# The head rows of batch 0 through two hardware DMA queues in a rotary-embedding kernel

## The chip, the cores and the metric

The kernel runs on one core of a Trainium2 chip. A core has compute engines that run their own instruction streams (VectorE, ScalarE, GpSimd, also called POOL, and SyncE, also called SP, which only issues transfers and waits; TensorE isn't used here) and 16 DMA engines that move data between the device memory (DRAM) and the on-chip memory (SBUF, 128 partitions). An engine's instruction stream issues a transfer into its queue and goes on; the DMA engines do the moving. The metric is the device time of one launch in microseconds (us), the median of several runs.

## The reference

The kernel applies a rotary position embedding. `x` is 8 x 2048 x 16 x 64 (batch, sequence, heads, head size), float32, 67.1 MB; `cos` and `sin` are 2048 x 32, 0.26 MB each. The output has the shape and type of `x`.

```python
x1 = x[..., :head_dim // 2]
x2 = x[..., head_dim // 2:]
cos = cos[None, :, None, :]
sin = sin[None, :, None, :]
out1 = x1 * cos - x2 * sin
out2 = x1 * sin + x2 * cos
return np.concatenate([out1, out2], axis=-1)
```

## The kernel before

One batch is one tile. The 2048 positions lie on 128 partitions, `J` = 16 consecutive positions ("rows" of 16 x 64 values) on each, so a partition's share of a batch is one contiguous piece of 64 KB in DRAM. Tiles are float16: a load through POOL's queue (line 52) casts float32 to float16 on the way, and a store (lines 60, 100, 130, 132) casts back. [...] There are five tile buffers for eight batches.

The first two rows of batch 0 (`JA` = 2) take another way. They come in as float32 through SP's queue into the tile `head`, 128 partitions x 8 KB (line 36), and ScalarE copies them, cast, into the first tile (line 84). The load of batch 0 on POOL's queue brings rows 2 to 15 alone. Behind the head, SP's queue carries `sin` and `cos` (lines 44 and 45), 2 KB per partition each. ScalarE turns sin into float16 with both signs (lines 88 and 89) and cos into float16 (line 90).

`rotate` is three VectorE instructions on a stretch of rows: the products of the swapped halves with sin into `v` (line 73), the products with cos in place (line 79), and their sum (line 81). It runs for rows 0 and 1 of batch 0 first, then rows 2 to 15, then for the seven other batches.

The order in POOL's queue is partly written out with dependencies between instructions: the loads of batches 0 to 3, then the store of row 0 of batch 0 (line 100), then the load of batch 4, the store of the rest of batch 0 (line 60), and from there stores and the loads of batches 5 to 7. A load into a used buffer waits for the store of what lay in it. Transfers of one queue take their turn in the order of issue on each DMA engine.

The last batch leaves in three parts: rows 0 to 8 (line 130) and 9 to 13 (line 132) through POOL's queue, and the last two rows through SP's: ScalarE copies them to float32 in `head`, used a second time (line 140), and SP stores them (line 141) once the part of line 130 has landed.

The change touches lines 36 to 39 of the kernel before. ScalarE's instruction stream there has six instructions that count as work and issues no transfer.

Of the kernel before, what the change touches and what calls it, by code (L numbers as in the profile page):

```python
# [1 line left out]

# [4 lines left out]


@with_exitstack  # L10
def kernel(
    ctx: ExitStack,
    tc: tile.TileContext,
    x: bass.AP,
    cos: bass.AP,
    sin: bass.AP,
    out: bass.AP,
):
    nc = tc.nc
    f16 = mybir.dt.float16  # L20
    f32 = mybir.dt.float32

    B, S, H, D = x.shape
    Dh = D // 2
    P = nc.NUM_PARTITIONS
    J = S // P
    NBUF = 5

    const_pool = ctx.enter_context(tc.tile_pool(name="rope_const", bufs=1))
    io_pool = ctx.enter_context(tc.tile_pool(name="rope_io", bufs=NBUF))  # L30
    tmp_pool = ctx.enter_context(tc.tile_pool(name="rope_tmp", bufs=1))

    JA = 2
    head = const_pool.tile([P, JA, H, D], f32)
    x0 = x[0].rearrange("(p j) h d -> p j (h d)", j=J)
    nc.sync.dma_start(  # L36
        out=head.rearrange("p j h d -> p (j h d)"),
        in_=x0[:, 0:JA, :].rearrange("p j f -> p (j f)"),
    )
    sin_f = const_pool.tile([P, J, Dh], f32)  # L40
    cos_f = const_pool.tile([P, J, Dh], f32)
    cos_h = const_pool.tile([P, J, Dh], f16)
    sin_h = const_pool.tile([P, J, D], f16)
    nc.sync.dma_start(out=sin_f, in_=sin.rearrange("(p j) d -> p j d", j=J))  # L44
    nc.sync.dma_start(out=cos_f, in_=cos.rearrange("(p j) d -> p j d", j=J))

    loads = []

    def load(b):
        xt = io_pool.tile([P, J, H, D], f16)  # L50
        j0 = JA if b == 0 else 0
        dma = nc.gpsimd.dma_start(  # L52
            out=xt[:, j0:J, :, :].rearrange("p j h d -> p (j h d)"),
            in_=x[b].rearrange("(p j) h d -> p j (h d)", j=J)[:, j0:J, :].rearrange("p j f -> p (j f)"),
        )
        loads.append(dma)
        return xt

    def store(b, xt, j0=0):
        return nc.gpsimd.dma_start(  # L60
            out=out[b].rearrange("(p j) h d -> p j (h d)", j=J)[:, j0:J, :].rearrange("p j f -> p (j f)"),
            in_=xt[:, j0:J, :, :].rearrange("p j h d -> p (j h d)"),
        )

    def rotate(xt, j0, j1):
        v = tmp_pool.tile([P, J, H, D], f16)
        n = j1 - j0
        js = slice(j0, j1)
        shape = [P, n, H, 2, Dh]
        sin_b = sin_h[:, js, :].rearrange("p j (e d) -> p j e d", e=2).unsqueeze(2).to_broadcast(shape)  # L70
        cos_b = cos_h[:, js, :].unsqueeze(2).to_broadcast([P, n, 2 * H, Dh])
        xe = xt[:, js, :, :].rearrange("p j h (e d) -> p j h e d", e=2)
        nc.vector.tensor_mul(  # L73
            out=v[:, js, :, :].rearrange("p j h (e d) -> p j h e d", e=2),
            in0=xe[:, :, :, ::-1, :],
            in1=sin_b,
        )
        xw = xt[:, js, :, :].rearrange("p j h (e d) -> p j (h e) d", d=Dh)
        nc.vector.tensor_mul(out=xw, in0=xw, in1=cos_b)  # L79
        xa = xt[:, js, :, :].rearrange("p j h d -> p (j h d)")  # L80
        nc.vector.tensor_add(out=xa, in0=xa, in1=v[:, js, :, :].rearrange("p j h d -> p (j h d)"))  # L81

    tiles = [load(b) for b in range(NBUF - 1)]
    nc.scalar.copy(  # L84
        out=tiles[0][:, 0:JA, :, :].rearrange("p j h d -> p (j h d)"),
        in_=head.rearrange("p j h d -> p (j h d)"),
    )
    nc.scalar.copy(out=sin_h[:, :, Dh:D], in_=sin_f)  # L88
    nc.scalar.mul(out=sin_h[:, :, 0:Dh], in_=sin_f, mul=-1.0)  # L89
    nc.scalar.copy(out=cos_h, in_=cos_f)  # L90
    rotate(tiles[0], 0, JA)
    def part(b, j0, j1):
        return (
            out[b].rearrange("(p j) h d -> p j (h d)", j=J)[:, j0:j1, :].rearrange("p j f -> p (j f)"),
            tiles[b][:, j0:j1, :, :].rearrange("p j h d -> p (j h d)"),
        )

    def store_rows(b, j0, j1):
        dst, src = part(b, j0, j1)
        return nc.gpsimd.dma_start(out=dst, in_=src)  # L100

    first = store_rows(0, 0, 1)
    tc.add_manual_dep(
        first.ins,
        loads[NBUF - 2].ins.name,
        mybir.DependencyInfo(mybir.DependencyClass.NoSync, mybir.DependencyReason.DATA),
        reason="order of the ring",
    )
    tiles.append(load(NBUF - 1))
    tc.add_manual_dep(  # L110
        loads[NBUF - 1].ins,
        first.ins.name,
        mybir.DependencyInfo(mybir.DependencyClass.NoSync, mybir.DependencyReason.DATA),
        reason="order of the ring",
    )
    for b in range(B):
        rotate(tiles[b], JA if b == 0 else 0, J)
        if b < B - 1:
            st = store(b, tiles[b], 1 if b == 0 else 0)
            if b == 0:  # L120
                tc.add_manual_dep(
                    st.ins,
                    first.ins.name,
                    mybir.DependencyInfo(mybir.DependencyClass.NoSync, mybir.DependencyReason.DATA),
                    reason="order of the ring",
                )
        if b + NBUF < B:
            tiles.append(load(b + NBUF))
    dst, src = part(B - 1, 0, 9)
    gate = nc.gpsimd.dma_start(out=dst, in_=src)  # L130
    dst, src = part(B - 1, 9, J - JA)
    rest = nc.gpsimd.dma_start(out=dst, in_=src)  # L132
    tc.add_manual_dep(
        rest.ins,
        gate.ins.name,
        mybir.DependencyInfo(mybir.DependencyClass.NoSync, mybir.DependencyReason.DATA),
        reason="order of the ring",
    )
    dst, src = part(B - 1, J - JA, J)
    nc.scalar.copy(out=head.rearrange("p j h d -> p (j h d)"), in_=src)  # L140
    end = nc.sync.dma_start(out=dst, in_=head.rearrange("p j h d -> p (j h d)"))
    tc.add_manual_dep(
        end.ins,
        gate.ins.name,
        mybir.DependencyInfo(mybir.DependencyClass.Sync, mybir.DependencyReason.DATA),
        reason="the last rows go out behind this part",
    )


# [1 line left out]
_INS = ['x', 'cos', 'sin']  # L151
_OUTS = [((8, 2048, 16, 64), 'float32')]


# [23 lines left out]
```

## Time and profile before

| what | value |
|---|---|
| time, median of 3 runs | 316.88 us (316.84 to 317.36) |
| span of the profiled execution, first to last instruction | 315.7 us |
| time around the span (median less span) | 1.2 us |
| VectorE busy | 209.1 us |
| ScalarE busy | 6.8 us |
| POOL busy | 9.9 us |
| HBM read and written | 67.63 MB and 67.11 MB |
| head: issue to landing | 4.8 us |
| sin and cos: issue to landing | 13.5 and 32.0 us |
| four loads of x at the start, issued by POOL | 1.25 to 3.51 us |

The time of the profiled execution itself is known only as its span. In the lines of a profile, times are in us from the start of the span unless marked ns. "SPq" and "POOLq" are the issuing streams of SyncE and GpSimd. A line of the order of time gives start, length, engine, source line and operation, and in brackets the idle time ahead of it and what ended that. L36 is line 36 of the kernel. The picture of 40 slices shows a busy share in tenths (9 is 90% or more). In a table by stretches, columns are the stretch, its length, the busy time of VectorE, ScalarE and POOL with instruction counts, the TensorE clock, the mean busy share of the 16 DMA engines and GB/s. Bytes count as they are written at the destination; a load counts as float16, a store as float32. A transfer is made of packets, here one for each partition and a small one for each engine that reports completion.

### The profile page before, as it was taken

The page shows a single profiled execution, that of the slowest core. Times are in us where ns is not written, and L with a number is a line of the kernel's source. Part 1 is how long each engine was busy: PE and PEld are TensorE (multiplying, and loading weights), DVE is VectorE, ACT ScalarE, POOL GpSimd, SP SyncE. Part 2 cuts the span into 40 slices and gives each one's busy share as a digit, 9 for nine tenths or more (in the row PEclk, how much of TensorE's full clock was granted, in tenths as well). Part 3 has the DMA queues.
Part 4 walks back from the last instruction along what each step waited for, and adds up shares of the span by engine and source line. Part 5 has one row for each costly group of instructions (what it writes and reads, how often), then busy time and mean ns, then how long its engine had stood idle before and what let it go on. Part 6 is the DMA issues. An engine that isn't in the chain of part 4 may idle for free.

```text
span 315.7 us, 122 instructions
## 1 busy us (share of the span) xinstructions
DVE 209.1 (66%) x27; ACT 6.8 (2%) x6; POOL 9.9 (3%) x22
## 2 busy tenths in 40 slices
DVE  0010699999999999999999999994009994000000
ACT  4100000000000000000000000000000002000000
POOL 3000100000000000001000000100000001000000
DMA  9899999999999989999999999999999999999998
GB/s 277 183 262 208 199 220 245 199 199 199 266 199 199 498 374 523 399 332 241 224 199 199 390 407 399 399 531 266 199 249 482 399 399 515 415 399 399 432 434 330
DMA packets 3168, 101.71 MB, mean 322 GB/s; under 512 B 352, under 2 KB 352, under 8 KB 736
## 3 DMA queue, kind: packets, MB, share of 16 engines
q0 software_dynamic: 2592, 99.09, 98.1%
q1 hardware_dynamic: 576, 2.62, 2.3%
HBM read 67.63 MB, written 67.11 MB: 427 GB/s over the span
## 4 chain that ended last, share of the span: by engine, by line
DVE 25%; DMA 22%; issue 18%; another core or an unknown queue 17%; POOL 1%; ACT 1%; SPq 0%; POOLq 0%; DVEq 0%; ACTq 0%
DMA xt<-in_x_dram 12%; DMA cos_f<-in_cos_dram 10%; DVE xt L79 8%; DVE xt L81 8%; DVE v L73 8%; ACT head L140 1%; POOL out_dram L60 1%; POOL xt L52 0%; ACT cos_h L90 0%; SPq L44 0%; SPq L36 0%; POOLq L52 0%; POOLq L60 0%; DVEq L73 0%
## 5 line engine op out<-in xcount | busy, mean ns | idle before, releaser
L73 DVE TENSOR_TENSOR v<-xt,sin_h 128x16384 f16<-128x16384 f16 (+2 forms) x9 | 69.7, 7744 | 36.8 <-DMA xt<-in_x_dram 20.7
L79 DVE TENSOR_TENSOR xt<-xt,cos_h 128x16384 f16<-128x16384 f16 (+2 forms) x9 | 69.7, 7744 | 17.5 <-ACT cos_h L90 17.2
L81 DVE TENSOR_TENSOR xt<-xt,v 128x16384 f16<-128x16384 f16 (+2 forms) x9 | 69.7, 7744 | 0.3
L52 POOL DMA_DIRECT2D xt<-in_x_dram x8 | 4.4, 557 | 111.1 <-DMA out_dram<-xt 110.3
L140 ACT CAST head<-xt 128x2048 f32<-128x2048 f16 x1 | 1.9, 1897 | 229.5 <-DVE xt L81 229.5
L60 POOL DMA_DIRECT2D out_dram<-xt x7 | 3.7, 535 | 63.9 <-DVE xt L81 63.9
L130 POOL DMA_DIRECT2D out_dram<-xt x1 | 0.5, 531 | 46.3 <-DVE xt L81 46.3
L84 ACT CAST xt<-head 128x2048 f16<-128x2048 f32 x1 | 1.9, 1897 | 3.6 <-DMA head<-in_x_dram 3.6
L100 POOL DMA_DIRECT2D out_dram<-xt x1 | 0.5, 541 | 33.5 <-DVE xt L81 33.5
L84 ACT ACT_TABLE_LOAD x1 | 1.3, 1283 | 0.7 <-PEq L162 0.7
L90 ACT CAST cos_h<-cos_f 128x512 f16<-128x512 f32 x1 | 0.6, 618 | 17.8 <-DMA cos_f<-in_cos_dram 17.8
L88 ACT CAST sin_h<-sin_f 128x512 f16<-128x512 f32 x1 | 0.6, 617 | 7.2 <-DMA sin_f<-in_sin_dram 7.2
L89 ACT ACTIVATE sin_h<-sin_f 128x512 f16<-128x512 f32 x1 | 0.6, 624 | 0.0
L132 POOL DMA_DIRECT2D out_dram<-xt x1 | 0.5, 531 | 0.0
L162 POOL MEMSET const-float32-0.0<- 128x1 f32 x1 | 0.1, 99 | 0.2 <-issue 0.2
L162 POOL MEMSET const-bfloat16-1.0<- 128x1 bf16 x1 | 0.1, 102 | 0.0
L162 POOL MEMSET const-float32-1.0<- 128x1 f32 x1 | 0.1, 99 | 0.0
L162 POOL MEMSET const-uint8-127<- 128x1 uint8 x1 | 0.1, 99 | 0.0
## 6 DMA issues: line engine op xcount, KB each, us to landing
xt<-in_x_dram POOLq DMA_DIRECT2D x7, 4096.0 KB, 41.3
out_dram<-xt POOLq DMA_DIRECT2D x1, 7680.0 KB, 61.6
out_dram<-xt POOLq DMA_DIRECT2D x1, 4608.0 KB, 42.4
xt<-in_x_dram POOLq DMA_DIRECT2D x1, 3584.0 KB, 22.3
out_dram<-xt POOLq DMA_DIRECT2D x1, 2560.0 KB, 47.9
head<-in_x_dram SPq DMA_DIRECT2D x1, 1024.0 KB, 4.8
out_dram<-head SPq DMA_DIRECT2D x1, 1024.0 KB, 8.4
out_dram<-xt POOLq DMA_DIRECT2D x1, 512.0 KB, 47.1
```

Source lines behind the costliest of these rows:

```text
L52: dma = nc.gpsimd.dma_start(out=xt[:, j0:J, :, :].rearrange("p j h d -> p (j h d)"), in_=x[b].rearrange("(p j) h d -> p j (h d)", j=J)[:, ...
L60: return nc.gpsimd.dma_start(out=out[b].rearrange("(p j) h d -> p j (h d)", j=J)[:, j0:J, :].rearrange("p j f -> p (j f)"), in_=xt[:, j0:J ...
L73: nc.vector.tensor_mul(out=v[:, js, :, :].rearrange("p j h (e d) -> p j h e d", e=2), in0=xe[:, :, :, ::-1, :], in1=sin_b,)
L79: nc.vector.tensor_mul(out=xw, in0=xw, in1=cos_b)
L81: nc.vector.tensor_add(out=xa, in0=xa, in1=v[:, js, :, :].rearrange("p j h d -> p (j h d)"))
L84: nc.scalar.copy(out=tiles[0][:, 0:JA, :, :].rearrange("p j h d -> p (j h d)"), in_=head.rearrange("p j h d -> p (j h d)"),)
L88: nc.scalar.copy(out=sin_h[:, :, Dh:D], in_=sin_f)
L89: nc.scalar.mul(out=sin_h[:, :, 0:Dh], in_=sin_f, mul=-1.0)
L90: nc.scalar.copy(out=cos_h, in_=cos_f)
L100: return nc.gpsimd.dma_start(out=dst, in_=src)
L130: gate = nc.gpsimd.dma_start(out=dst, in_=src)
L140: nc.scalar.copy(out=head.rearrange("p j h d -> p (j h d)"), in_=src)
```

## The change

The load of `head` is cut in two by partitions. The lower half, partitions 0 to 63, stays where it was at the front of SP's queue. The upper half, partitions 64 to 127, is issued by ScalarE into ScalarE's own queue, ahead of ScalarE's copy of the head in the program. Destination tile, bytes and row length are the same; the copy of line 84 needs both halves. Nothing else is edited.

```diff
     head = const_pool.tile([P, JA, H, D], f32)
     x0 = x[0].rearrange("(p j) h d -> p j (h d)", j=J)
     nc.sync.dma_start(
-        out=head.rearrange("p j h d -> p (j h d)"),
-        in_=x0[:, 0:JA, :].rearrange("p j f -> p (j f)"),
+        out=head[0:64].rearrange("p j h d -> p (j h d)"),
+        in_=x0[0:64, 0:JA, :].rearrange("p j f -> p (j f)"),
+    )
+    nc.scalar.dma_start(
+        out=head[64:128].rearrange("p j h d -> p (j h d)"),
+        in_=x0[64:128, 0:JA, :].rearrange("p j f -> p (j f)"),
     )
     sin_f = const_pool.tile([P, J, Dh], f32)
     cos_f = const_pool.tile([P, J, Dh], f32)
```

## The prediction

> **What bounds the kernel now.** I read the 40-slice picture first, then the DMA queues, and then the order of time on every engine; the chain of waits comes last, because it ends in "another core or an unknown queue" and "issue" for a third of the span and so doesn't name the resource. From the page:
>
> ```profile
> span 315.7 us, 122 instructions
> DVE 209.1 (66%) x27; ACT 6.8 (2%) x6; POOL 9.9 (3%) x22
> ...
> DMA  9899999999999989999999999999999999999998
> ...
> DMA packets 3168, 101.71 MB, mean 322 GB/s; under 512 B 352, under 2 KB 352, under 8 KB 736
> ...
> q0 software_dynamic: 2592, 99.09, 98.1%
> q1 hardware_dynamic: 576, 2.62, 2.3%
> HBM read 67.63 MB, written 67.11 MB: 427 GB/s over the span
> ```
>
> The DMA row is 8 or 9 in every slice: the 16 DMA engines are busy from end to end, VectorE only for 66%. The two queues together hold 98.1% + 2.3% = 100.4% of the engines' time; it can exceed 100 because packets of different queues overlap. The bytes are fixed by the problem, so the time is (67.63 + 67.11) MB at the rate that the engines hold, and an edit can gain only where they stand idle or lose only where it makes them slower. The change touches q1, which is 2.62 of 101.71 MB. The packet counts also say how a transfer is spread: the program has 22 transfers (4 on SP, 18 on POOL), 22 x 128 = 2816 packets are one per partition, and the 352 left, all under 512 B, are 22 x 16, one completion write per engine. So each transfer, those of SP's queue among them, uses all 16 engines, 8 rows on each.
>
> The start, where the change is. Order of time, then the busy share of the DMA engines in short stretches (the last two columns are DMA share and GB/s; a packet is booked in full when it ends, so a share over 1 is a packet that began earlier):
>
> ```profile
> 0.74 1.28 ACT L84 ACT_TABLE_LOAD   x1 [0.74 <-PEq L162]
> 0.74 0.37 SPq L36 DMA_DIRECT2D head<-in_x_dram  x1
> 1.16 0.42 SPq L44 DMA_DIRECT2D sin_f<-in_sin_dram  x1
> 1.25 2.26 POOL L52 DMA_DIRECT2D xt<-in_x_dram  x4 [0.81 <-PEq L173]
> 1.63 0.42 SPq L45 DMA_DIRECT2D cos_f<-in_cos_dram  x1
> 5.58 1.90 ACT L84 CAST xt<-head 128x2048 f16<-128x2048 f32 x1 [3.56 <-DMA head<-in_x_dram]
> 14.68 0.62 ACT L88 CAST sin_h<-sin_f 128x512 f16<-128x512 f32 x1 [7.20 <-DMA sin_f<-in_sin_dram]
> ```
>
> ```profile
> 1.50:3.00 1.50, 0.00 (x0) 0.52 (x1) 1.50 (x4) 1.00 0.83 186
> 3.00:5.00 2.00, 0.00 (x0) 0.00 (x0) 0.51 (x1) 1.00 0.98 401
> 5.00:6.00 1.00, 0.00 (x0) 0.42 (x1) 0.00 (x0) 1.00 2.54 616
> ```
>
> The head's issue ends at 1.11 us and the head has landed at 5.58. From 1.5 to 3.0 us the engines move 186 GB/s, from 3 to 5 us 401: there is a ramp. From 5 us on the large packets of POOL's queue end in waves, the first in 5 to 6 us, and the engines never rest again.
>
> **The change part by part.**
>
> SP's queue. The one issue of 128 rows (0.37 us) becomes one of 64 rows. Nothing in the trace shows a 64-row issue; its bounds are 0 and the 0.37 us of the 128-row one. The sin issue beside it has the same 128 rows of a quarter of the bytes and takes 0.42, so rows or the fixed part set it, not bytes; I take 0.37. Sin and cos are issued at 1.16 and 1.63 as before, or up to 0.37 us earlier.
>
> ScalarE's queue. One new issue, 0.35 to 0.42 us by the four issues on SP (0.37, 0.42, 0.42 and the 0.35 of the last rows), with nothing ahead of it but, at the worst, the table load of 1.28 us. Behind it on ScalarE stand the table load and the copy of the head (line 84), which waits until 5.58 us anyway: 0.74 + 0.42 + 1.28 = 2.44 us, so 3.1 us of idle time cover the issue. The copy now waits for two transfers in place of one. POOL's queue is not passed by anything: its four loads still take 1.25 to 3.51 us.
>
> DMA work. The same bytes in the same 128 rows of 8 KB, and 16 more completion writes: packets 3168 + 16 = 3184, if a 64-row transfer uses all 16 engines too. The row of the hardware queue, 2.3% in 576 packets, gives 0.023 x 16 x 315.7 / 576 = 0.2 us of one engine for a packet on average, data rows of 2 and 8 KB among them; one more per engine costs 0.2 us at that price, and nothing at the lower end. I take 0, since these packets carry hardly any data.
>
> When head, sin and cos land. In the large-packet stretch SP's queue gets about one row per POOL packet: cos follows sin by 33.63 - 14.68 = 18.95 us, 2.37 us for each of its 8 rows per engine, and the waves of POOL packets are some 2.2 us apart. With two hardware queues an engine takes a row from each between large packets. So the head should land at 5.6 us or one wave sooner, sin and cos in the same place or one or two waves (2 to 5 us) sooner; or, if ScalarE's rows come late, up to 4 rows x 2.37 = 9.5 us later for the upper half of the head. None of that reaches the end. Line 84 feeds the first rotation, and VectorE then runs without a gap from 34.28 to 216.8 us. The first store leaves POOL at 37.06 us, but in POOL's queue it stands behind four loads of 16.3 MB (as written, 3584 + 3 x 4096 KB), which at 217 GB/s (34 to 80 us) fill the engines until about 80: 43 us of cover. The store of batch 0 is issued at 60.0 us and its turn comes at about 102. At the other end, VectorE is done at 263.7 us while older stores keep the engines full until about 292: 28 us of cover. Shifts of -5 to +9.5 us vanish in these; were that cover gone, the shift would come through one to one.
>
> What can reach the end is the engines' own busy time in the first 6 us.
> - Gain. At the 401 GB/s of the next stretch, the 186 GB/s x 1.5 us = 279 KB of the ramp take 0.70 us, so at most 0.80 us is to be had there. Two queues that each bring a first row to every engine can fill the pause between the first and the second row. But the large packets that end in 5 to 6 us have been read beside the head's rows: by 6 us SP's queue has brought the head and 190 KB of sin (1.24 MB) and POOL's 16 packets of 57 KB read (0.92 MB), and 2.16 MB at the 427 GB/s of the span are 5.1 us, so measured this way work began at 0.9 us and there is no ramp left to win. The ends are 0 and 0.80 us. I take 0.2, near the second reckoning, which counts both queues.
> - Loss. A 64-partition transfer is not in this trace. If the two halves disturb each other so far that they run at half rate, the head's 1.05 MB at 401 GB/s, 2.6 us, become 5.2: +2.6 us. If they don't, 0. I take 0: in the final stretch, 306 to 314 us, SP's last rows and POOL's run in turn on the same engines at 405 GB/s against 435 in the 14 us before, so queues side by side cost there at most 7% of what they move, which for 2.6 us is 0.2 us. A gain from side by side is already in the item above.
>
> Sum: -0.2 us of ramp, 0 for completion writes, 0 for ScalarE, 0 for the landings: 315.5 us of span. The profiled execution has its span, 315.7; the timed runs lie at 316.84 to 317.36 with the median at 316.88, so 1.2 us lie around the span, which I leave alone: 316.7 us.
>
> [...]
>
> **The rivals.**
> 1. The ramp is won in full. For it: 186 against 401 GB/s from 1.5 to 3.0 us, a hole that more rows in flight could fill, and an engine-bound kernel passes such a gain on to its end. Against it: the 2.16 MB by 6 us. 316.88 - 0.80 = 316.1 us.
> 2. Slower: the halves collide. The place is 1.5 to 6 us, where three queues (POOL's, SP's and ScalarE's) have rows for the same engines and each engine's rows of one half all go to one half of the partitions. The price is up to 2.6 us, 319.5; at half of that, +1.3, 318.2. It decides over 0.2% from 0.63 us on, a quarter of the head's transfer time. Against it: the 405 against 435 GB/s at the end, though there both transfers span 128 partitions.
> 3. The change doesn't do what it says: ScalarE's issue comes behind its table load, at 2.02 us, and its rows start at about 2.8 us, when most of SP's half has gone. The halves then run one after the other. SP's next rows, sin's, fill the engines, so nothing is idle that was not: 316.9, with the head later and sin sooner.
> 4. The start or end of a launch costs more with a second hardware queue in use, in the 1.2 us around the span or before the first issue. Nothing in the trace shows that price. Its bounds are 0 and, by the nearest row, the whole 1.2 us once more: 318.1.
>
> **How the numbers follow.** Measurements of this kernel tell about 0.2%, 0.63 us, from no change (its three times span 0.52 us). The forecast with small effects of either sign, rival 3 among them, has 0.52 and stays within 0.63 us. Rival 1, a gain over 0.63 us, needs nearly all the ramp, or more than I can see in it: 0.19. Rival 2 gets 0.22 and rival 4 0.07. So faster 0.19, same 0.52, slower 0.29. The low end, 315.9, takes in the ramp's 0.80 us and the spread of the runs; the high end, 318.4, takes in half the price of a collision and all of rival 4; beyond them I leave about 0.04 and 0.10. The forecast alone would be 316.25 to 317.5.
>
> **What would show it.** Right: 3184 packets, 16 more of them under 512 B; the DMA row still 9 throughout; an issue on ScalarE's queue at 0.74 us; the head landed at 5 to 6 us; the first wave of large packets still in 5 to 6 us; sin at 10 to 15 us; VectorE's start moved, and no wait of POOL longer than before by more than the shift of the DMA. Rival 1: the stretch from 1.5 to 3.0 us near 400 GB/s and every later wave 0.6 to 0.8 us earlier. Rival 2: fewer than 401 GB/s from 3 to 5 us, and the first wave after 6 us. Rival 3: the issue at 2.0 us. Rival 4: an unchanged span and a longer time. The prediction is wrong altogether if the rate of the large packets changes far from the start, in a stretch that the edit doesn't touch, or if one engine gets more rows than the others (a half on 8 engines: completion writes 352 or fewer).

## The result and the profile after

The changed kernel takes 318.78 us (318.76 to 318.84), the kernel before 316.88 us in the runs beside it: a ratio of 1.0059 with a 95% interval of 1.0048 to 1.007, slower by 1.9 us. Repeated later it was 318.31 against 317.03 us, 1.0033 (1.002 to 1.0046), slower by 1.3 us. The lower ends of the two intervals, 0.48% and 0.2%, lie above and at the 0.2% that the prediction called a difference. 316.7 us was forecast.

The page of the changed kernel, the lines that answer to those shown of before:

```profile
span 317.0 us, 126 instructions
...
DMA  9899999999999999999999999999999999999997
...
DMA packets 3184, 101.71 MB, mean 321 GB/s; under 512 B 368, under 2 KB 368, under 8 KB 752
...
q0 software_dynamic: 2592, 99.09, 97.3%
q1 hardware_dynamic: 512, 2.10, 2.1%
q10 hardware_dynamic: 80, 0.52, 0.7%
HBM read 67.63 MB, written 67.11 MB: 425 GB/s over the span
```

The engines are still busy throughout, and the packet counts are the predicted ones (3184, 368 of them small). But the hardware queues, q1 and the new q10, now hold 2.1% + 0.7% = 2.8% of the engines' time for the same 2.62 MB that took 2.3% before. The same bytes occupy the engines longer. "ACTq" is ScalarE's issuing stream, and from line 40 on the changed kernel's lines are numbered four higher. Order of time at the start, and the stretches:

```profile
0.74 0.54 SPq L36 DMA_DIRECT2D head<-in_x_dram  x1
0.74 0.55 ACTq L40 DMA_DIRECT2D head<-in_x_dram  x1
1.25 2.26 POOL L56 DMA_DIRECT2D xt<-in_x_dram  x4 [0.80 <-PEq L177]
1.34 0.56 SPq L48 DMA_DIRECT2D sin_f<-in_sin_dram  x1
1.96 0.42 SPq L49 DMA_DIRECT2D cos_f<-in_cos_dram  x1
5.91 1.28 ACT L88 ACT_TABLE_LOAD   x1 [5.91 <-DMA head<-in_x_dram]
8.29 1.90 ACT L88 CAST xt<-head 128x2048 f16<-128x2048 f32 x1 [1.10 <-DMA head<-in_x_dram]
19.20 0.62 ACT L92 CAST sin_h<-sin_f 128x512 f16<-128x512 f32 x1 [9.01 <-DMA sin_f<-in_sin_dram]
```

```profile
1.50:3.00 1.50, 0.00 (x0) 0.00 (x0) 1.50 (x4) 1.00 0.61 104
3.00:5.00 2.00, 0.00 (x0) 0.00 (x0) 0.51 (x1) 1.00 1.01 258
5.00:6.00 1.00, 0.00 (x0) 0.09 (x1) 0.00 (x0) 1.00 1.12 254
```

From 3 to 5 us the DMA share is 1.01, as before (0.98), but 258 GB/s move in place of 401: busy and slow. The head's copy begins at 8.29 us instead of 5.58, sin's at 19.20 instead of 14.68.

The trace also records each packet with its start and duration. Worked out from those records (they don't name the engine, so rows are taken in order of start, 16 at a time, about one for each engine): in the kernel before, a row of the head takes 0.31 us once the first wave is past, and all rows are done at 5.19 us. In the changed kernel SP's rows begin at 2.06 us (before: 1.73). The first of an engine's four rows takes 0.9 us, the second 0.31, the third 0.5 and the last 0.62. ScalarE's begin at 4.08, when the first engines have finished SP's rows, take 0.48 to 0.65 us, and end at 7.44. The rows of sin right behind them, though they go to all 128 partitions, take 0.16 us each instead of 0.08. As the first engines come to the end of the head and of a few rows of sin, POOL's first large packet begins: at 7.18 us, before it was 5.28. Everything behind it stands in one queue that never empties; the store of the last part is issued 1.28 us later than before (line 145 at 307.71, line 141 at 306.43).

The two shifts, 1.9 us of POOL's first packet and 1.3 us of the last store, differ because of something else in the trace of before. Its POOL load packets of 32 KB take 2.43 us, but some before 84 us take more, 1.03 us in sum for each engine, half of it in the last wave of the fourth load, near 79 us. The changed kernel has 0.02 us of this. The view by stretches, before and then the changed kernel, shows the place: fewer packets begin from 77 to 82 us in the kernel before.

```profile
77.00:82.00 5.00, 4.97 (x2) 0.00 (x0) 0.00 (x0) 1.00 0.66 118
```

```profile
77.00:82.00 5.00, 4.97 (x2) 0.00 (x0) 0.00 (x0) 1.00 0.97 210
```

One wave of difference says little in itself, since a packet counts where it starts; the durations carry the reading.

All packets together close the account, in us for each engine. Those of the hardware queues take 9.04 in place of 7.13, 1.9 more (the head's rows 4.64 for 3.09, those of sin and cos 1.81 for 1.47). The first row comes 0.3 later. POOL's packets take 308.6 in place of 309.6, 1.0 less. That sums to 1.2 us, against the 1.3 us by which the span grew.

### The profile page after: what moved, and what is told of

Its sections match the earlier page's. It is cut to its first block, busy times and chain, and to the rows that moved or that the text cites. A ratio compares the mean times of both kernels' runs of the same rounds, so it can differ in the third digit from the quotient of the medians.

```text
span 317.0 us, 126 instructions
## 1 busy us (share of the span) xinstructions
DVE 209.1 (66%) x27; ACT 6.8 (2%) x6; POOL 9.9 (3%) x22
## 2 busy tenths in 40 slices
DMA packets 3184, 101.71 MB, mean 321 GB/s; under 512 B 368, under 2 KB 368, under 8 KB 752
## 4 chain that ended last, share of the span: by engine, by line
DVE 24%; DMA 24%; issue 18%; another core or an unknown queue 16%; POOL 1%; ACT 1%; SPq 0%; POOLq 0%; DVEq 0%; ACTq 0%
DMA xt<-in_x_dram 12%; DMA cos_f<-in_cos_dram 11%; DVE xt L85 8%; DVE xt L83 8%; DVE v L77 8%; ACT head L144 1%; POOL out_dram L64 1%; POOL xt L56 0%; ACT cos_h L94 0%; SPq L48 0%; SPq L36 0%; POOLq L56 0%; POOLq L64 0%; DVEq L77 0%
```

## The experiments

Two theories at first. **H**: a transfer into one half of the partitions moves at about half the rate, and the large packets wait behind it. **Q**: two hardware queues with rows at the same time cost the time. Here is what the runs share, one trace for each kernel, all from the packet records: the median duration of all rows of the head, the first wave with them (SP's / ScalarE's, in e1 the lower half / the upper half), the median start of POOL's first 16 packets, the sum of slowed load packets (POOL packets of 20 KB or more that start before 84 us, what they take beyond the 10th percentile of their size, divided by the 16 engines), the start of the 673rd POOL packet, early in the fifth load, and that start less the slowed packets. Differences in the last column are thus delays made at the start. The first 16 alone don't give them, since more or fewer rows of the hardware queues can go ahead of that wave.

```
kernel                     row of head, us    first 16   slowed  673rd   673rd less slowed
before                     0.31               5.42       1.03    88.12   87.09
changed                    0.57 / 0.61        7.60       0.02    89.22   89.20
e5 changed, again          0.58 / 0.61        7.40       0.02    89.12   89.10
e1 halves, one queue       0.52 / 0.32        4.31       0.28    88.00   87.72
e2 by row, two queues      0.16 / 0.16 (4 KB) 5.35       0.49    87.53   87.04
e3 even and odd            0.35 / 0.31        5.45       0.69    87.92   87.23
e4 whole on ScalarE        0.31               5.56       0.80    87.80   87.00
e11 the same, again        0.31               5.57       0.30    87.38   87.08
e6 lower half alone        0.58               5.43       0.03    86.80   86.77
e7 middle half alone       0.32               3.99       0.21    86.44   86.23
e8 one row, whole          0.16 (4 KB)        4.31       0.77    87.89   87.12
e9 one row, halves         0.17 / 0.27 (4 KB) 5.18       0.09    87.99   87.90
e10 sin in halves          0.31               5.12       0.77    87.67   86.90
```

**Both halves on one queue.**

```diff
-nc.scalar.dma_start(
+nc.sync.dma_start(
     out=head[64:128].rearrange("p j h d -> p (j h d)"),
```

> Both halves are issued on SP's queue, the lower one first; ScalarE issues nothing. Theory H (a transfer into one half of the partitions moves at about half the rate, whichever queue carries it): slow like the changed kernel, 318.2 to 318.8 us, rows of 8 KB at about 0.6 us each, the first POOL packet about 1.6 to 1.9 us later than in the kernel before (one more issue on SP, 0.4 us, included). Theory Q (rows on two hardware queues at once cost the time: slower issues, a later first row, switching): 316.9 us, at most 0.3 more for the additional issue.

317.47 us (317.1 to 318.05), ratio 1.001 (1.0 to 1.0019): neither theory's number in microseconds. Against the 317.26 us of the kernel before in the same rounds it is 0.2 us more, which Q allowed and H did not. The issues:

```profile
0.74 0.55 SPq L36 DMA_DIRECT2D head<-in_x_dram  x1
1.25 2.26 POOL L56 DMA_DIRECT2D xt<-in_x_dram  x4 [0.80 <-PEq L177]
1.35 0.57 SPq L40 DMA_DIRECT2D head<-in_x_dram  x1
...
17.11 1.28 ACT L88 ACT_TABLE_LOAD   x1 [17.11 <-DMA head<-in_x_dram]
18.40 1.90 ACT L88 CAST xt<-head 128x2048 f16<-128x2048 f32 x1
```

The first half slows to 0.6 us a row from 3.5 us on, as H says, with one queue. But POOL's first packet then comes in at 3.76 us, and the second half goes out one row to each large packet, at 0.32 us, until 14.6 us. So the head lands 9 us later than in the changed kernel, and the launch is 0.8 us faster than the 318.31 us of its second measurement. So the head's lateness is not what costs. It fits slow rows that stand in front of POOL's packets with nothing to share the engines: in the change both halves did, here only one (0.63 us in the last column against 2.1).

**Cut by rows instead of partitions, two queues.**

```diff
-    out=head[0:64].rearrange("p j h d -> p (j h d)"),
+    out=head[:, 0:1].rearrange("p j h d -> p (j h d)"),
...
-    out=head[64:128].rearrange("p j h d -> p (j h d)"),
+    out=head[:, 1:2].rearrange("p j h d -> p (j h d)"),
```

> The same megabyte through the same two queues, but cut by rows: SP brings row 0 and ScalarE row 1, each on all 128 partitions in pieces of 4 KB. Theory H: the head moves at about 400 GB/s as in the kernel before, and only the later first row is left, 316.9 to 317.3 us. Theory Q: slow like the changed kernel, 318.4 to 318.8 us.

317.31 us, ratio 1.0002 (0.9993 to 1.0011): no loss. Its stretches:

```profile
1.50:3.00 1.50, 0.00 (x0) 0.00 (x0) 1.50 (x4) 1.00 0.73 197
3.00:5.00 2.00, 0.00 (x0) 0.00 (x0) 0.51 (x1) 1.00 1.01 391
```

The engines take rows of the two queues in turn from 2.35 us on, at 391 GB/s. Theory Q falls: two queues side by side are here as fast as one (391 GB/s against 401 in the kernel before).

**Even and odd partitions, two queues.**

```diff
-    out=head[0:64].rearrange("p j h d -> p (j h d)"),
+    out=head[0:128:2].rearrange("p j h d -> p (j h d)"),
...
-    out=head[64:128].rearrange("p j h d -> p (j h d)"),
+    out=head[1:128:2].rearrange("p j h d -> p (j h d)"),
```

> Two halves of 64 partitions in rows of 8 KB on the same two queues as in the change, but SP takes the even partitions and ScalarE the odd ones, so that each half is spread over all of the memory. If which partitions form a half is the cause (theory H in its narrow form), the rows take 0.31 to 0.4 us and the time is 316.9 to 317.4 us. If any 64-row transfer is slow (8 rows per engine becoming 4, or any skipping of partitions), or by theory Q: 318.4 to 318.8 us.

317.23 us, ratio 1.0002 (0.9993 to 1.0011). It has the same two queues, the same 64 rows of 8 KB in each, the same late first row (2.06 us), and ScalarE's rows again mostly after SP's. Only which partitions are in a half differs:

```profile
0.74 0.55 ACTq L40 DMA_DIRECT2D head<-in_x_dram  x1
0.74 0.54 SPq L36 DMA_DIRECT2D head<-in_x_dram  x1
```

```profile
1.50:3.00 1.50, 0.00 (x0) 0.00 (x0) 1.50 (x4) 1.00 0.67 186
3.00:5.00 2.00, 0.00 (x0) 0.52 (x1) 0.51 (x1) 1.00 0.94 388
```

388 GB/s against the change's 258, at issues as long as the change's. That is the sharpest of the runs: which partitions form a half is the cause.

**The whole head on ScalarE's queue.**

```diff
-    nc.sync.dma_start(
+    nc.scalar.dma_start(
         out=head.rearrange("p j h d -> p (j h d)"),
```

> The whole head, 128 partitions, on ScalarE's queue; sin and cos stay on SP's. Two hardware queues are in use, but no transfer is cut. Theory H: the head moves at the full rate, 316.6 to 317.3 us; sin, now first on SP's queue, lands earlier. Theory Q: 317.5 us or more, since head and sin rows come through two queues at once; if a second hardware queue itself has a price outside the span, time less span is larger here than in the kernel before by that price.

317.07 us, ratio 0.9993 (0.9983 to 1.0002). ScalarE's queue has no price, and time less span is 317.37 - 315.6 = 1.8 us, as in a run without it (317.45 - 315.7 for the whole head of one row).

**The change again.** The edit is the change itself.

> The changed kernel as it is, beside the runs of the next two on one chip. If its loss belongs to the kernel and not to a chip: 318.6 to 319.0 us, rows of 8 KB near 0.6 us, the first POOL packet about 1.9 us later than in the kernel before.

318.31 us (318.17 to 318.46), ratio 1.0033 (1.002 to 1.0046), a little under the expected range. Its rows and first wave are as in the first trace: SP's at 0.58, ScalarE's at 0.61 (medians), POOL's first packet at 7.18 us.

**Half of the head alone, lower or middle.** Both leave the other 64 partitions of the head unloaded and zero, so half a megabyte of the work is missing.

```diff
-    out=head.rearrange("p j h d -> p (j h d)"),
-    in_=x0[:, 0:JA, :].rearrange("p j f -> p (j f)"),
+    out=head[0:64].rearrange("p j h d -> p (j h d)"),
+    in_=x0[0:64, 0:JA, :].rearrange("p j f -> p (j f)"),
 )
+nc.vector.memset(head[64:128].rearrange("p j h d -> p (j h d)"), 0.0)
```

> Only the lower half of the head, partitions 0 to 63, is loaded, on SP's queue; the upper half is set to zero by VectorE and never loaded, so half a megabyte of work is left out. [...]

The middle half has [32:96] in both places, and zeros in [0:32] and [96:128].

> Only partitions 32 to 95 of the head are loaded, on SP's queue, as many rows in one piece as in the lower half alone; the others are set to zero by VectorE, and half a megabyte of work is left out. [...]

316.23 us (316.05 to 316.28) for the lower half, 315.84 (315.59 to 317.01) for the middle one. The stretch from 3 to 5 us, lower half first (in the middle one POOL's first packets already begin in it):

```profile
3.00:5.00 2.00, 0.00 (x0) 0.00 (x0) 0.51 (x1) 1.00 1.04 219
```

```profile
3.00:5.00 2.00, 1.55 (x1) 0.22 (x1) 0.51 (x1) 1.00 1.48 389
```

Rows of the lower half take 0.62 us from 3.5 us on, those of the middle half 0.32: the position of the 64 rows makes a factor of two in their duration, in single unbroken transfers on one queue. So a half is slow by itself, with no other half to disturb it. In time it is 0.4 us. My estimate by theory H was 0.9 to 1.3, since half the rate loses again most of what the missing bytes save, 0.52 MB / 401 GB/s = 1.3 us; for two halves that move alike it was at most 0.3. So the time hardly tells the two apart, and the factor of two rests on the rows. The last column has 0.54. It fits the rest of the miss that the lower half isn't slow throughout: its rows in order of start, 16 at a time, take 0.61, 0.32, 0.50 and 0.63 us, those of the middle half 0.65, 0.32, 0.31 and 0.32.

The middle half also settles a rival on the reading side in part: its rows come from as long and dense a stretch of DRAM as those of the lower half. But in every run with a slow head, the rows of partitions 0 to 63 come from the first half of the batch's bytes and those of 64 to 127 from the second, so no run separates a limit at the partitions from one at these two stretches of DRAM.

**A head of one row.**

```diff
-JA = 2
+JA = 1
```

> The kernel before with a head of one row (4 KB a partition) in place of two; the last store through SP's queue is one row too. It is the base of the next run. Any theory: 316.5 to 317.8 us.

> The changed kernel with a head of one row, against the run with the whole head of one row. Theory H: the part of the loss that goes with the bytes is halved, from 1.6 to 0.8 us, and 0.3 us of a later first row stay: 0.9 to 1.4 us more than the whole. If the loss is a fixed price of 64-row transfers or of the second queue: 1.7 to 2.1 us more, as with two rows.

The whole took 317.45 us, the halves 317.28 (ratios to the kernel before 1.0005 and 0.9997): no loss, a clear miss of both theories. The packets of the two traces give a reason. ScalarE's rows do slow down, from 0.16 us to 0.2 to 0.3, and the start is later by 87.90 - 87.12 = 0.78 us. But the whole has 0.77 us of slowed packets and the halves 0.09, which nearly cancels it. Why the one has them and the other not is the question of the next run.

**Do slow rows at the start prevent the slowed packets later?** Four traces with the half-rate rows (the change twice, the lower half alone, the one-row halves) have under 0.1 us of these packets, the others up to then 0.2 to 1.03, among them the run with both halves on one queue (0.28), whose first half is slow too.

```diff
-nc.sync.dma_start(out=sin_f, in_=sin.rearrange("(p j) d -> p j d", j=J))
+sin_p = sin.rearrange("(p j) d -> p j d", j=J)
+nc.sync.dma_start(out=sin_f[0:64], in_=sin_p[0:64])
+nc.sync.dma_start(out=sin_f[64:128], in_=sin_p[64:128])
```

> The kernel before with sin instead of the head cut into partitions 0 to 63 and 64 to 127, both on SP's queue behind the whole head; one more issue. Theory H prices it: 0.26 MB at half the rate would cost at most 0.26 MB / 401 GB/s = 0.65 us, and less as sin's rows stand between POOL packets. Question left open by the runs so far: kernels with a half-rate stage at the start show no slowed POOL load packets up to 84 us, the others 0.2 to 1.0 us of them per engine. If a half-rate stage as such prevents them: under 0.1 us of slowed packets, runs within 0.4 us of each other, 316.5 to 317.0 us. If it is something else: 0.2 to 1.0 us of them as in the kernel before, runs spread over about 1 us, 317.0 to 317.9 us.

317.27 us (316.7 to 318.4), 0.77 us of slowed packets in its trace: a transfer by halves as such does not prevent them. But sin's rows took 0.08 to 0.1 us here as in the kernel before, so there was no half-rate stage, and whether one prevents slowed packets is not tested. What slows those packets, and why the change's traces lack them, stays open. It is not what made the change slower: the change has fewer of them. It hides a part of the loss, and may do so differently from run to run.

**The whole head on ScalarE's queue, more rounds.** The edit is that of the first such run.

> The whole head on ScalarE's queue again, with more rounds, because its first ratio, 0.9993 with an interval of 0.9983 to 1.0002, leaves a gain open. If sin's rows beside the head's fill the first microseconds better: 316.7 to 317.1 us and a ratio below 1. If not: a ratio of 1.000 within 0.0005.

316.82 us (316.65 to 317.39) against 317.35, ratio 0.9983 (0.9975 to 0.9992): with the first run's 0.9993 a small gain, and the fastest version here that does the whole work. Sin's rows now run between the head's:

```profile
0.74 0.39 ACTq L36 DMA_DIRECT2D head<-in_x_dram  x1
0.74 0.38 SPq L44 DMA_DIRECT2D sin_f<-in_sin_dram  x1
...
7.69 0.62 ACT L88 CAST sin_h<-sin_f 128x512 f16<-128x512 f32 x1 [5.25 <-DMA sin_f<-in_sin_dram]
10.21 1.90 ACT L84 CAST xt<-head 128x2048 f16<-128x2048 f32 x1 [1.90 <-DMA head<-in_x_dram]
```

(from the first of the two runs). By the last column of the table the start is earlier than in the kernel before by 0.1 us or less. The rest of the 0.5 us isn't shown to come from the start; the two traces have fewer slowed packets (0.80 and 0.30 us against 1.03).

## Why the prediction was wrong

- **The frame held.** The kernel is bound by the DMA engines, 16 engines serve each transfer (3184 packets, 368 small), and a later head, sin or cos costs nothing: sin was 4.5 us later than before in the change, and in the one-queue run, which took 0.2 us more, the head was 11.5 us later and sin 21.6.
- **The step that failed is the loss item, "If they don't, 0. I take 0".** It should have been about 2 us: the last column moves from 87.09 to 89.20 and 89.10, of which even and odd partitions on the same two queues, 87.23, leave 1.9 to 2.0 us to the choice of the halves. The 2.6 us named there as the upper end, each half at half rate, was nearly right. Rival 2 had the place, the price and the signs (258 GB/s from 3 to 5 us, the first wave after 6 us), but not the mechanism. It and the loss item let the two halves disturb each other; the lower half alone, on one queue, is just as slow (0.58 us a row in the median, SP's rows in the change 0.57), and in the change the halves hardly ran side by side (SP's rows from 2.06 us on, ScalarE's from 4.08). What decided against it was a row that doesn't bear on it: the last rows at 405 against 435 GB/s are two transfers over all 128 partitions. It showed that queues share engines well, which the run by rows confirms (391 GB/s), and nothing of a half of the partitions. I should have taken a value between the ends, with the upper end reaching the time.
- **The price of a half was missing from the sum.** A row takes 0.62 us in the lower half alone, 0.32 in the middle one and 0.31 with even and odd partitions behind the first wave. So the position of the rows makes a factor of two; the traces don't show by what. That the halves share the 16 engines doesn't explain the loss, since the even and odd halves share them as well and cost nothing (ratio 1.0002). What rate two halves like those of the change reach when they run at once, no run shows.
- **A column was misread.** "A packet is booked in full when it ends" is wrong. The packet records put the first POOL packet's start at 5.28 us, just where the share rises: a packet counts where it begins. So the 0.92 MB "read beside the head's rows" had only begun by 6 us, and the argument that no ramp is left falls with it. The ramp was not won all the same: with the first rows at 2.06 us it became longer, 104 GB/s against 186, and the 0.2 us of gain in the sum did not come.
- **The issue was mis-sized.** "I take 0.37" for 64 rows; it is 0.54 and 0.55, ScalarE's above the 0.35 to 0.42 us expected for it, and the first row comes 0.33 us later. In the run with even and odd partitions that lateness stood alone and cost 87.23 - 87.09 = 0.14 us of the start.
- **ScalarE's rows.** "An engine takes a row from each between large packets" was right for the cut by rows, 128 partitions each (in turn from 2.35 us on, at 391 GB/s). In the change SP's four rows came first and then ScalarE's four, so the halves did not cover each other, and POOL got no turn between (its first packet began at 7.18 us). Rival 3 had the halves one after another, but with the wrong reason (the table load; the issue was at 0.74 us) and a price of nothing, 316.9 us.
- **Time around the span.** 1.2 us was the median less the profiled span. Every run that lists both has 1.7 to 1.8 us, so the profiled execution of before was probably one of about 317.5 us, above the median. That also fits the 1.3 us between the two spans, which is less than the 1.9 us between the medians. Rival 4 is out: the figure is the same with and without ScalarE's queue.
- **Far from the start.** The sum had no term for the slowed load packets near 79 us, though the prediction named a change there as a sign that it was wrong. They moved the other way: 1.0 us of the loss is hidden by them in the trace.

## What to carry to other kernels

If such a transfer is to be cut, cut it by bytes within the partitions, or by partitions spread over the whole range (ratios of 1.0002 here), and not into partitions 0 to 63 and 64 to 127 (1.0059 and 1.0033). Where one queue never empties, ask of an early transfer not when it lands but how long it holds the engines before the large packets get their turn: here a head 11.5 us later went with 0.2 us, and a first large packet 1.9 us later with 1.3 and 1.9 us. A comparison row must share the property in dispute: two queues at full width (405 GB/s at the end, 391 in the run by rows) say nothing of one at half width (258).

## What the hardware showed unexpectedly

- Issues of 64 rows took longer than most of 128 rows: 0.53 to 0.60 us against 0.36 to 0.44, on one queue as on two. But 128-row issues behind them were long too (sin's 0.56 in the change, cos's up to 0.65 in other runs), so the number of rows is not all of it.
- Slowness builds up: in the change the second row of an engine still took 0.31 us, the third 0.5, the last 0.62, and sin's rows behind the head were slowed with it.
- In the change, on a second queue, all of an engine's four rows went ahead of POOL's packets (the first began at 7.18 us), while in the one-queue run a second transfer on the same queue let POOL in at 3.76 us.
- Nine of the 13 traces lose 0.2 to 1.03 us to slowed load packets, half or more of it in one wave near 79 us, and the runs of the kernel before spread over about 1.1 us; the change's traces have 0.02 us, and its runs spread over 0.1 to 0.3 us. The cause is open.
